# ConvFFN of a two-layer hybrid encoder: 19 of 22 up-projection column pairs by Strassen's seven block products, the down projection as a phase of its own

## The chip, the cores and the metric

The kernel runs on one core of a Trainium2 chip. The metric is the device time of one execution in microseconds, as the median of several runs. Five engines work side by side, each through its own list of instructions in a fixed order: TensorE (PE, with its weight loads shown as PEld), VectorE (DVE), ScalarE (ACT), GpSimd (POOL) and SyncE (SP). Semaphores tie them together. Matmuls write PSUM, which has eight banks of 512 columns of fp32; the other engines read them from there.

## The reference

Two layers run over 1024 prompt tokens and 64 sample tokens (1088 in all), width 1024. Each layer has a mixer (gated linear attention beside differential attention) and a causal ConvFFN. The change is in the second half of each layer:

```python
x = x + rms_norm(mix, ln_mix_post)
h = rms_norm(x, ln_ffn_pre)
up = h @ w_ffn_up                        # 1024 -> 2 x 2816
ext = jnp.concatenate([conv_state.astype(up.dtype), up], axis=1)
c = conv_b
for i in range(CONV_W):                  # 3 taps along the tokens
    c = c + conv_w[i] * ext[:, i:i + T]
g, u = jnp.split(c, 2, axis=-1)
y = jax.nn.gelu(g, approximate=True) * u
x = x + rms_norm(y @ w_ffn_down, ln_ffn_post)   # 2816 -> 1024
```

## The kernel before

Activations are kept feature-major: a tile holds 128 features on the partitions and tokens along the free axis. The residual stream and the sums of the down projection live in `ACC` (8 slices k of 128 features x 1088 tokens). Every product is computed as three passes of rounded fp32 parts: high by high, high by low, low by high. So each operand exists twice: `XH`/`XL` for x, `MH`/`ML` for the gated rows y, `WH`/`WL` for four slots of weights. A raw weight block (512 KB) lands in one of two halves of `RAW`; ACT rounds it into `WH`, DVE subtracts for `WL`.

`fm_block` makes 128 output features for one of three token groups (384, 384, 320 tokens): 8 slices x 3 passes = 24 matmuls into one PSUM bank. The up projection has 22 pairs j of such column blocks, a gate block and a value block (s = 0, 1). In the loop at the end of each layer, up pairs alternate with down products: after every second pair, `dn_mms` multiplies the y of two pairs by their rows of `w_ffn_down` (8 blocks m x 3 groups x 6 matmuls), and `ev_dn` adds the result into `ACC`. The last such product takes pairs 18 to 21 and is followed by the norm that ends the layer.

`ffn_step` evicts one up block and advances the two before it: the block leaves PSUM times `RB` (the inverse root mean square of each token, spread over the partitions), the first tap of the convolution runs on ACT, the other two on DVE, gelu on ACT, the gating on DVE, then y is split into `MH` and `ML`.

`chain(l, g, which, tag)` is the residual and norm work of a token group. With which = 1 it stands between the mixer's output projection and the up projection: `ACC` times `RB` plus residual, then `XH`, `XL` and the squares in `SQ`. x goes into the product without its inverse root mean square; `x_norm` computes that meanwhile (`ssum`: three small matmuls `ONE,SQ`; `rstd`: ACT, then a power on POOL; `bcast`: three small matmuls `IDN,RS`; ACT copies to `RB`), and the first blocks of a group are evicted up to five blocks late (`behind`) so that it is ready.

The order of everything is settled when the program is written out: `defer` evicts a block after the next block's matmuls, `pump` takes steps of waiting generators (`beside`, `soon`) by a modelled clock, `need` and `drain` take as many steps at once as are needed, `want` rounds weights. On the chip each engine runs its list as it stands. The helper lines 103 (matmul), 107 (transpose) and 122 (DVE) stand for nearly all instructions of their engines; in the changed file they are 110, 114 and 129.

## Time and profile before

| what | value |
|---|---|
| median of three runs | 2812.64 us (2810.19 to 2818.26) |
| profiled execution | 2810.27 us, span 2808.5 us |
| PE busy | 2766.1 us, 98% of the span |
| DVE busy | 1690.2 us, 60% |
| ACT busy | 1151.0 us, 41% |
| POOL busy | 234.8 us, 8% |
| DMA | 235.46 MB, mean 84 GB/s |
| granted PE clock, first-layer feed-forward | 1.00 |

Busy time is summed over the engine's instructions; a share is of the span. The profile's page gives these, the chain of work that ended last, and groups of instructions by line, operation and tile. The timeline lists single instructions or runs of equal ones with start, length, engine, line, operation, tiles written and read, and count; in brackets stands the idle time ahead of it and what ended it.

### The profile page before, as it was taken

What the parts mean: (1) busy time and instruction counts of PE and PEld (TensorE: products, weight loads), DVE (VectorE), ACT (ScalarE), POOL (GpSimd) and SP (SyncE); (2) the same over time, 40 slices, a digit from 0 to 9 for tenths busy, and PEclk for the clock granted to TensorE, in tenths of its full rate; (3) what the DMA queues carried; (4) which work ended last, traced back from release to release, by engine and by line L of the source; (5) the groups of instructions that cost most, each with busy time, mean ns of one, the idle gap of its engine ahead of it and who ended that gap; (6) DMA issues with size and microseconds to landing.
All of it is one profiled execution on the core that took longest, in us unless ns stands there. A gap on an engine that the chain in (4) does not pass through costs nothing.

```text
span 2808.5 us, 46577 instructions
## 1 busy us (share of the span) xinstructions
PE 2766.1 (98%) x18407; PEld 2710.2 (96%) x18407; DVE 1690.2 (60%) x4104; ACT 1151.0 (41%) x2432; POOL 234.8 (8%) x387
## 2 busy tenths in 40 slices
PE   8999999999999999999999999999999999999999
PEld 8999988999999999999999999889999999999999
DVE  5443458477566666666772433674766666666665
ACT  5334348555322222222454242684552222222235
POOL 2200024200000000000021001340000000000000
PEclk9999999999999999999999999999999999999999
DMA  7421175341111111111362213734311111111122
GB/s 252 137 70 46 58 195 144 117 135 57 46 46 42 42 45 46 46 46 46 109 199 85 62 39 106 203 93 131 122 56 42 42 45 46 46 46 46 46 91 84
DMA packets 250689, 235.46 MB, mean 84 GB/s; under 512 B 12974, under 2 KB 225416, under 8 KB 250472
## 3 DMA queue, kind: packets, MB, share of 16 engines
q1 hardware_dynamic: 233032, 189.62, 23.6%
q0 software_dynamic: 10656, 39.07, 4.0%
q10 hardware_dynamic: 6784, 3.81, 0.5%
q8 instruction: 145, 2.38, 0.4%
q14 instruction: 72, 0.59, 0.1%
HBM read 174.34 MB, written 58.11 MB: 83 GB/s over the span
## 4 chain that ended last, share of the span: by engine, by line
PE 92%; DMA 2%; DVE 2%; issue 2%; ACT 1%; POOL 0%; SPq 0%; ACTq 0%; DVEq 0%; POOLq 0%
PE PS L103 89%; PE PS L107 3%; DVE SML L122 1%; DMA out_dram<-TMP 1%; DVE ACC L122 1%; DMA WH<-QSd 0%; ACT ACC L1070 0%; DMA WH<-KSd 0%; DMA VSd<-TMP 0%; DMA QSd<-MH 0%; DVE TMP L122 0%; ACT WH L275 0%; DVE ML L122 0%; SPq L992 0%; DMA ACC<-in_x_prompt_dram 0%
## 5 line engine op out<-in xcount | busy, mean ns | idle before, releaser
L103 PE MATMUL PS<-XL,WH 128*128 128x384 f32 (+1 forms) x2976 | 558.6, 326 | 0.0
L103 PEld LDWEIGHTS PS<-XL,WH 128*128 128x128 f32 x2976 | 500.7, 188 | 0.0
L103 PE MATMUL PS<-XH,WH 128*128 128x384 f32 (+1 forms) x2592 | 484.9, 328 | 2.8 <-DVE TMP L122 2.8
L103 PE MATMUL PS<-XH,WL 128*128 128x384 f32 (+1 forms) x2592 | 480.0, 326 | 0.0
L103 PEld LDWEIGHTS PS<-XH,WH 128*128 128x128 f32 x2592 | 434.1, 188 | 4.0 <-DVE TMP L122 3.7
L103 PEld LDWEIGHTS PS<-XH,WL 128*128 128x128 f32 x2592 | 434.6, 188 | 0.2
L103 PE MATMUL PS<-MH,WH 128*128 128x384 f32 (+1 forms) x1248 | 387.3, 329 | 0.0
L103 PE MATMUL PS<-MH,WL 128*128 128x384 f32 (+1 forms) x1248 | 385.1, 327 | 0.0
L103 PE MATMUL PS<-ML,WH 128*128 128x384 f32 (+1 forms) x1248 | 384.3, 327 | 0.0
L122 DVE TENSOR_TENSOR TMP<-PS,RB 128x384 f32<-128x384 f32 (+2 forms) x376 | 159.5, 444 | 343.6 <-PE PS L103 329.4
L275 ACT ACTIVATE WH<-RAW 128x1024 fp32r<-128x1024 f32 (+2 forms) x209 | 216.7, 1048 | 336.4 <-PE PS L103 301.3
L1237 ACT ACTIVATE TMP<-TMP,VC 128x384 f32<-128x384 f32 (+1 forms) x264 | 183.1, 693 | 404.4 <-DVE TMP L122 403.6
L122 DVE TENSOR_TENSOR ACC<-PS,ACC 128x384 f32<-128x384 f32 (+1 forms) x456 | 239.6, 533 | 133.6 <-PE PS L103 132.9
L122 DVE TENSOR_TENSOR WL<-RAW,WH 128x1024 fp32r<-128x1024 f32 (+2 forms) x209 | 253.7, 1215 | 99.2 <-ACT WH L275 99.1
L122 DVE SCALAR_TENSOR_TENSOR TMP<-TMP,VC 128x384 f32<-128x384 f32 (+1 forms) x528 | 311.5, 590 | 0.1
L103 PEld LDWEIGHTS PS<-MH,WL 128*128 128x128 f32 x1248 | 230.9, 188 | 0.0
L103 PEld LDWEIGHTS PS<-ML,WH 128*128 128x128 f32 x1248 | 230.9, 188 | 0.0
L103 PEld LDWEIGHTS PS<-MH,WH 128*128 128x128 f32 x1248 | 230.1, 188 | 0.7 <-issue 0.3
L103 PE MATMUL PS<-WH,XH 128*128 128x256 f32 (+1 forms) x864 | 128.8, 292 | 0.0
L122 DVE TENSOR_REDUCE SML<-PS 128x1 f32<-128x384 f32 (+6 forms) x144 | 104.1, 724 | 40.4 <-PE PS L103 38.8
L103 PE MATMUL PS<-WH,XL 128*128 128x256 f32 (+1 forms) x864 | 122.7, 285 | 0.0
L1258 ACT ACTIVATE MH<-TMP 128x384 fp32r<-128x384 f32 x132 | 67.0, 508 | 135.5 <-DVE TMP L122 135.4
(202 smaller groups left out, 3420.3 us busy)
## 6 DMA issues: line engine op xcount, KB each, us to landing
RAW<-in_w_ffn_up_dram SPq DMA_DIRECT2D x88, 512.0 KB
RAW<-in_w_in_dram SPq DMA_DIRECT2D x48, 512.0 KB
RAW<-in_w_ffn_down_dram SPq DMA_DIRECT2D x44, 512.0 KB
RAW<-in_w_out_dram SPq DMA_DIRECT2D x32, 512.0 KB
XH<-XS SPq DMA_DIRECT2D x8, 1536.0 KB
XS<-ACC POOLq DMA_DIRECT2D x6, 1536.0 KB, 6.8
XH<-KSd SPq DMA_DIRECT2D x32, 256.0 KB
XH<-XS SPq DMA_DIRECT2D x4, 1280.0 KB
```

Of the source, the lines that this page charges most:

```text
L103: nc.tensor.matmul(out, lhsT, rhs, **kw)
L107: nc.tensor.transpose(out, in_, idn)
L122: return op(out, *a, **kw)
L275: act(hi, src, AF.Copy)
L1237: act(c, e[:, 0:w], AF.Identity, bias=cb(l, u), scale=cw(l, 0, u))
L1258: act(MH[:, mid["j"] % 4, mid["t0"]:mid["t0"] + n], y[:, :n], AF.Copy)
```

## The change

Three of 22 pairs (j = 0, 1, 2) keep the plain blocks. For the other 19, the 1024 x 256 weights of a pair (gate and value columns) are taken as a 2 x 2 block matrix (features 0 to 511 and 512 to 1023, gate and value), x as a 2 x 2 block matrix (the same feature halves; tokens 0 to 543 and 544 to 1087), and the product is made from seven block products (Winograd's form of Strassen's scheme) in place of eight. Each product is two halves of 272 tokens x 12 matmuls. The sums of weight blocks (four per pair) are made on DVE (`prep`), the sums of x's blocks once per layer (`fresh`, `late_split`), the sums of products in the evictions (`evict`).

The sums need x with its norm applied, so `chain` with which = 1 now makes two passes: the first for residual and squares, then a wait for `x_norm`, then x times weight and `RB`, rounded by ACT, low part by DVE. The eviction of an up block is a plain copy on ACT. The gated rows go to DRAM (`YD`) from POOL's queue. The down projection follows all up products: five rounds over 4, 4, 4, 3 and 3 pairs (`part_mms`, weights of one m in units of 256 or 192 KB), y read back and split, then the last part over pairs 18 to 21 as before.

```diff
+NC = 3
+HT = T // 2
+Q = HT // 2
+NP = 7 * (NF - NC)
+SKIPS = (0, 1, 2)
+CHUNKS = ((0, 4), (4, 8), (8, 12), (12, 15), (15, 18))
...
+        for j in range(NC):
+            L["up", j] = fm_unit(w_ffn_up[l], j * 128, nxt())
+            fm_unit(w_ffn_up[l], FF + j * 128, nxt())
+        L["prod"] = [nxt() for _ in range(NP)]
+        for c, (ja, jb) in enumerate(CHUNKS):
+            for m in range(8):
+                L["dnc", c, m] = part_unit(w_ffn_down[l], ja, jb, m, nxt())
+            nxt(c in SKIPS)
+        held.update((L["dnc", 0, 0], L["dnc", 0, 1]))
+        for j in range(18, NF):
+            L["dn", j] = down_unit(w_ffn_down[l], j * 128, nxt())
...
+        if which == 1:
+            for k in range(8):
+                V.tensor_tensor(a(k), a(k), rb, ALU.mult)
+                V.scalar_tensor_tensor(a(k), a(k), ln(l, which, k), f(XH[:, k, t0:t0 + n]), ALU.mult, ALU.add)
+                if k > 1:
+                    V.tensor_tensor(sq, sq, sqb[:, (k - 1) % 2, :n], ALU.add)
+                act(sqb[:, k % 2, :n] if k else sq, a(k), AF.Square)
+                if k % 4 == 3:
+                    nc.gpsimd.dma_start(XS[:, k - 3:k + 1, t0:t0 + n], accv[:, k - 3:k + 1, t0:t0 + n])
+                if k == 7:
+                    V.tensor_tensor(sq, sq, sqb[:, 1, :n], ALU.add)
+                    soon(x_norm(), (tag, "rs", g))
+                yield
+            while (tag, "rs", g) not in done:
+                yield tag, "rs", g
+            def low(k):
+                x = XH[:, k, t0:t0 + n]
+                V.tensor_tensor(XL[:, k, t0:t0 + n], a(k), f(x), ALU.subtract)
+            for k in range(8):
+                V.scalar_tensor_tensor(a(k), a(k), ln(nl, nw, k), rb, ALU.mult, ALU.mult)
+                act(XH[:, k, t0:t0 + n], a(k), AF.Copy)
+                if k:
+                    low(k - 1)
+                if k == 7:
+                    low(7)
+                    done.add((tag, "x", g))
+                yield
+            return
...
-                V.tensor_tensor(e[:, 2:2 + n], PS[:, b, :n], RB[:, t0:t0 + n], ALU.mult)
+                act(e[:, 2:2 + n], PS[:, b, :n], AF.Copy)
...
-                act(MH[:, mid["j"] % 4, mid["t0"]:mid["t0"] + n], y[:, :n], AF.Copy)
-                mid["y"] = y
+                nc.gpsimd.dma_start(YD[mid["j"], :, mid["t0"]:mid["t0"] + n], y[:, :n])
...
+    def fresh(l):
+        for k in range(4):
+            b11, b12 = accv[:, k, :HT], accv[:, k, HT:]
+            b21, b22 = accv[:, k + 4, :HT], accv[:, k + 4, HT:]
+            V.tensor_tensor(b11, b12, b11, ALU.subtract)
+            act(MH[:, k, :HT], b11, AF.Copy)
+            yield
+            V.tensor_tensor(b12, b22, b12, ALU.subtract)
+            V.tensor_tensor(b22, b22, b11, ALU.subtract)
+            act(MH[:, k, HT:], b22, AF.Copy)
+            yield
+            V.tensor_tensor(ML[:, k, :HT], b11, f(MH[:, k, :HT]), ALU.subtract)
+            V.tensor_tensor(b21, b21, b22, ALU.subtract)
+            yield
+            V.tensor_tensor(ML[:, k, HT:], b22, f(MH[:, k, HT:]), ALU.subtract)
+            yield
+        done.add(("fresh", l))
...
+    def late_split(i):
+        k = i % 4
+        if i < 4:
+            src, hi, lo = accv[:, k, HT:], T3[:, 0, k], T3[:, 1, k]
+        else:
+            src, hi, lo = accv[:, k + 4, :HT], XH[:, k, HT:], XL[:, k, HT:]
+        act(hi, src, AF.Copy)
+        return lambda: V.tensor_tensor(lo, src, f(hi), ALU.subtract)
...
+        def prep(self, p):
+            n, i = divmod(p, 7)
+            if n >= self.n:
+                return
+            a, b = [r.rearrange("p (k c) -> p k c", k=8) for r in self.raw(n)]
+            a11, a12, a21, a22 = a[:, :4], a[:, 4:], b[:, :4], b[:, 4:]
+            s1, s2, s4, s3 = SG
+            src = (a11, s2, s1, s4, s3, a12, a22)[i]
+            if i == 1:
+                V.tensor_tensor(s1, a21, a22, ALU.add)
+                V.tensor_tensor(s2, s1, a11, ALU.subtract)
+            if i == 3:
+                V.tensor_tensor(s4, a12, s2, ALU.subtract)
+            if i == 4:
+                V.tensor_tensor(s3, a11, a21, ALU.subtract)
+            hi, lo = [x.rearrange("p (k c) -> p k c", k=4) for x in self.part(p)]
+            act(hi, src, AF.Copy)
+            self.lows[p] = (lo, src, f(hi))
+        def low(self, p):
+            if p in self.lows:
+                V.tensor_tensor(*self.lows.pop(p), ALU.subtract)
+        def rhs(self, i, k, hl, s):
+            X, M = (XH, XL)[hl], (MH, ML)[hl]
+            c = slice(s * Q, s * Q + Q)
+            d = slice(HT + s * Q, HT + s * Q + Q)
+            return (X[:, k, c], M[:, k, d], M[:, k, c], X[:, k + 4, d], T3[:, hl, k, c], X[:, k + 4, c], X[:, k, d])[i]
+        def mms(self, p):
+            n, i = divmod(p, 7)
+            w = self.part(p)
+            for s in range(2):
+                b = self.bank(p) + s
+                j = 0
+                for wl, hl in PASSES:
+                    for k in range(4):
+                        mm(PS[:, b, :Q], w[wl][:, k * 128:(k + 1) * 128], self.rhs(i, k, hl, s),
+                           start=j == 0, stop=j == 11)
...
+        def evict(self, p):
+            if p < 0:
+                return
+            n, i = divmod(p, 7)
+            b = self.bank(p)
+            out = PS[:, b:b + 2, :Q]
+            if i == 0:
+                act(two(P1S), out, AF.Copy)
+            elif i == 1:
+                V.tensor_tensor(two(U2S), out, two(P1S), ALU.add)
+            elif i == 2:
+                V.tensor_tensor(two(U4S), out, two(U2S), ALU.add)
+            elif i == 3:
+                self.second(0, b, U4S)
+            elif i == 4:
+                self.second(1, b, U4S)
+                V.tensor_tensor(two(U2S), out, two(U2S), ALU.add)
+            else:
+                s = i - 5
+                V.tensor_tensor(two(EB[s][:, 2:2 + HT]), out, two((P1S, U2S)[s]), ALU.add)
+                self.ends(s, n)
...
+        def conv(self, p):
+            n, i = divmod(p, 7)
+            if i == 6 and n < self.n:
+                self.tap(0, 0, n)
+            n -= 1
+            if n < 0 or i > 4:
+                return
+            if i == 0:
+                self.tap(1, 0, n)
+                self.tap(0, 1, n)
+            elif i == 1:
+                self.tap(0, 2, n)
+            elif i == 2:
+                act(CB[0], CB[0], AF.Gelu_apprx_tanh)
+                self.tap(1, 1, n)
+            elif i == 3:
+                self.tap(1, 2, n)
+            else:
+                y, c = CB
+                V.tensor_tensor(y[:, :SEQ], y[:, :SEQ], c[:, :SEQ], ALU.mult)
+                V.tensor_tensor(y[:, SEQ:T], y[:, SEQ + 2:T + 2], c[:, SEQ + 2:T + 2], ALU.mult)
+                nc.gpsimd.dma_start(YD[NC + n], y[:, :T])
...
+        blk = Blocks(l)
+        for j in range(2, NC):
+            for g in range(3):
+                for s in range(2):
+                    up_block(j, s, g)
+                    if j + 1 < NC:
+                        if g == 0:
+                            want(L["up", j] + 2 + s)
+                    elif (g, s) == (0, 0):
+                        blk.load(0)
+                    elif (g, s) == (1, 1):
+                        blk.prep(0)
+                    elif (g, s) == (2, 0):
+                        need(("fresh", l))
+                        drain()
+                        blk.low(0)
+                        blk.prep(1)
+                    pump(2)
+        blk.low(1)
+        blk.start()
+        for p in range(NP):
+            n, i = divmod(p, 7)
+            blk.mms(p)
+            if p == 0:
+                flush()
+                blk.load(1)
+                blk.prep(2)
+                blk.low(2)
+            elif p < 3:
+                ffn_step(l, None)
+            if p == 4:
+                for e in EB:
+                    V.memset(e[:, 0:2], 0.0)
+            blk.evict(p - 1)
+            blk.prep(p + 3)
+            blk.conv(p)
+            if p < 4:
+                lows2 = [late_split(2 * p), late_split(2 * p + 1)]
+                for x in lows2:
+                    x()
+            blk.low(p + 3)
+            if i == 4:
+                blk.load(n + 2)
+            if n == blk.n - 1:
+                d0 = L["dnc", 0, 0]
+                ys = TMP[:, 544:544 + T]
+                if i == 0:
+                    y_load(0, ys)
+                elif i == 3:
+                    y_high(0, ys)
+                    y_low(0, ys)
+                    y_load(3, ys)
+                elif i == 4:
+                    y_load(1, RB)
+                    y_load(2, SQ)
+                    held.difference_update((d0, d0 + 1))
+                    fetch(d0 + 1)
+                elif i == 5:
+                    want(d0)
...
+        left = [lambda: (blk.evict(NP - 1), blk.conv(NP))]
+        left += [lambda p=p: blk.conv(p) for p in range(NP + 1, NP + 5)]
+        for c, (ja, jb) in enumerate(CHUNKS):
+            nx = range(*CHUNKS[c + 1]) if c + 1 < len(CHUNKS) else range(18, NF)
+            for m in range(8):
                 for g in range(3):
-                    for s in range(2):
-                        up_block(j, s, g)
-                        if g == 0:
-                            want(n + 2 + s)
-            elif j < 18:
-                for m in range(8):
-                    for g in range(3):
-                        b = bank()
-                        dn_mms(b, j, (j, j + 1), m, g, True, True)
-                        defer(lambda m=m, g=g, b=b, j=j: ev_dn(j == 0, False, m, g)(b))
-                    if m in (1, 4):
-                        want(n + 2 + (m > 1))
+                    b = bank()
+                    part_mms(b, c, m, g)
+                    if left:
+                        left.pop(0)()
+                    defer(lambda m=m, g=g, b=b, c=c: ev_dn(c == 0, False, m, g)(b))
+                    if g == 0:
+                        want(L["dnc", c, m] + 2)
```

Three places in the order of instructions show what moved. The first is PE at the start of the up projection of token group 1, in layer 0. Names: `XH,WH` and the like are the passes of up blocks, `ONE,SQ` and `IDN,RS` the small products of `x_norm`. Before, from the third block of group 0:

```order
L103 MATMUL PS<-XH,WH 128x384 x8
L103 MATMUL PS<-XL,WH 128x384 x8
L103 MATMUL PS<-XH,WL 128x384 x8
L103 MATMUL PS<-ONE,SQ 128x1 x3
L103 MATMUL PS<-XH,WH 128x384 x8
L103 MATMUL PS<-XL,WH 128x384 x8
L103 MATMUL PS<-XH,WL 128x384 x8
L103 MATMUL PS<-IDN,RS 128x128 x3
L103 MATMUL PS<-XH,WH 128x384 x8
L103 MATMUL PS<-XL,WH 128x384 x8
L103 MATMUL PS<-XH,WL 128x384 x8
```

and now:

```order
L110 MATMUL PS<-XH,WH 128x384 x8
L110 MATMUL PS<-XL,WH 128x384 x8
L110 MATMUL PS<-XH,WL 128x384 x8
L110 MATMUL PS<-XH,WH 128x384 x8
L110 MATMUL PS<-XL,WH 128x384 x8
L110 MATMUL PS<-XH,WL 128x384 x8
L110 MATMUL PS<-ONE,SQ 128x1 x3
L110 MATMUL PS<-IDN,RS 128x128 x3
L110 MATMUL PS<-XH,WH 128x384 x8
L110 MATMUL PS<-XL,WH 128x384 x8
L110 MATMUL PS<-XH,WL 128x384 x8
```

The block that stood between the two small products of `x_norm` stands ahead of both, and the blocks behind them read `XH` and `XL` of the same group.

The second is DVE in the chain of token group 2. `ACC<-ACC,RB` and `ACC<-ACC,VC,XH` are the residual, `XL` the low part of x, `SQ` the squares, `TMP` the convolution's steps. Before, the chain stood among the evictions of group 0's blocks:

```order
L122 TENSOR_TENSOR ACC<-ACC,RB 128x320
L122 SCALAR_TENSOR_TENSOR ACC<-ACC,VC,XH 128x320
L122 SCALAR_TENSOR_TENSOR XL<-ACC,VC,XH 128x320
L122 TENSOR_TENSOR SQ<-SQ,TMP 128x320
L122 MEMSET TMP 128x2
L122 TENSOR_TENSOR TMP<-PS,RB 128x384
L122 SCALAR_TENSOR_TENSOR TMP<-TMP,VC 128x384
L122 COPY HALO<-TMP 128x2
L122 SCALAR_TENSOR_TENSOR TMP<-TMP,VC 128x384
L122 TENSOR_TENSOR ACC<-ACC,RB 128x320
L122 SCALAR_TENSOR_TENSOR ACC<-ACC,VC,XH 128x320
L122 SCALAR_TENSOR_TENSOR XL<-ACC,VC,XH 128x320
```

and now it begins behind the step for the third block of group 1 (the first three rows), in one piece of 36 rows of which these are the first:

```order
L129 COPY HALO<-TMP 128x2
L129 SCALAR_TENSOR_TENSOR TMP<-TMP,VC 128x384
L129 TENSOR_TENSOR TMP<-TMP 128x384
L129 TENSOR_TENSOR ACC<-ACC,RB 128x320
L129 SCALAR_TENSOR_TENSOR ACC<-ACC,VC,XH 128x320
L129 TENSOR_TENSOR ACC<-ACC,RB 128x320
L129 SCALAR_TENSOR_TENSOR ACC<-ACC,VC,XH 128x320
L129 TENSOR_TENSOR ACC<-ACC,RB 128x320
L129 SCALAR_TENSOR_TENSOR ACC<-ACC,VC,XH 128x320
L129 TENSOR_TENSOR SQ<-SQ,TMP 128x320
```

and these are where the second pass begins, behind the last squares:

```order
L129 SCALAR_TENSOR_TENSOR ACC<-ACC,VC,XH 128x320
L129 TENSOR_TENSOR SQ<-SQ,TMP 128x320 x2
L129 SCALAR_TENSOR_TENSOR ACC<-ACC,VC,RB 128x320 x2
L129 TENSOR_TENSOR XL<-ACC,XH 128x320
L129 SCALAR_TENSOR_TENSOR ACC<-ACC,VC,RB 128x320
L129 TENSOR_TENSOR XL<-ACC,XH 128x320
```

Each slice is handled in two passes, and no eviction stands between their rows.

The third is DVE ahead of the first block product; `ACC<-ACC 128x544` and `ML<-ACC,MH` are `fresh`, `WL<-RB,WL` is the low part of the first product's weights. Before, evictions of the up blocks of pair 2 stood here alone (`TMP<-PS,RB`), for example:

```order
L122 COPY TMP<-HALO 128x2
L122 TENSOR_TENSOR TMP<-PS,RB 128x384
L122 SCALAR_TENSOR_TENSOR TMP<-TMP,VC 128x384
L122 COPY HALO<-TMP 128x2
L122 TENSOR_TENSOR ML<-TMP,MH 128x384
L122 SCALAR_TENSOR_TENSOR TMP<-TMP,VC 128x384
```

and now, behind the step for the second block of group 1 of pair 2 (the first two rows), the end of `fresh` follows in one piece:

```order
L129 COPY HALO<-TMP 128x2
L129 SCALAR_TENSOR_TENSOR TMP<-TMP,VC 128x384
L129 TENSOR_TENSOR ACC<-ACC 128x544 x2
L129 TENSOR_TENSOR ML<-ACC,MH 128x544
L129 TENSOR_TENSOR ACC<-ACC 128x544
L129 TENSOR_TENSOR ML<-ACC,MH 128x544
```

and, after more of the same, up to the weights:

```order
L129 TENSOR_TENSOR ACC<-ACC 128x544 x3
L129 TENSOR_TENSOR ML<-ACC,MH 128x544
L129 TENSOR_TENSOR ACC<-ACC 128x544
L129 TENSOR_TENSOR ML<-ACC,MH 128x544
L129 TENSOR_TENSOR WL<-RB,WL 128x512
L129 TENSOR_TENSOR ACC<-SQ 128x4x128
L129 TENSOR_TENSOR ACC<-ACC,RB 128x4x128
L129 COPY TMP<-HALO 128x2
```

The weights' low part and the first weight sums (`128x4x128`) stand behind all of `fresh`.

215 lines of the change are left out of this document (143 added, 72 removed).

## The prediction

> **What bounds the kernel now.** I read the page's busy shares first, then the chain that ended last, then the stretch of one feed-forward part.
>
> ```profile
> PE 2766.1 (98%) x18407; PEld 2710.2 (96%) x18407; DVE 1690.2 (60%) x4104; ACT 1151.0 (41%) x2432; POOL 234.8 (8%) x387
> 527.56 834.85 PE PS L103 x5088
> 1910.04 834.92 PE PS L103 x5088
> core 0: us, PE busy (x) PEld busy (x) DVE busy (x) ACT busy (x) POOL busy (x), PEclk, DMA share, GB/s
> 613.76:1395.00 781.24, 780.80 (x4747) 780.34 (x4745) 515.75 (x1297) 257.96 (x412) 5.63 (x6) 1.00 0.18 53
> ```
>
> TensorE (PE) is busy 98% of the span. The two rows of the chain (start, length) are the output projection and feed-forward of each layer: 835 us with nothing on the chain but matmuls. In the window, the feed-forward of layer 0, PE stands still for 0.4 of 781 us, VectorE (DVE) works 66% of it and ScalarE (ACT) 33%. So a matmul saved there is time saved, and a PE that waits there is time lost. This execution took 2810.27 us (span 2808.5); the median of the three runs is 2812.64, 2.4 more.
>
> **What the products save.** The pitch of PE's instructions is read from the starts of the weight loads in the timeline (start, length, count at the end): first 384-column matmuls, then 320, and then the only stage with 272, the first value projection.
>
> ```profile
> 1003.25 1.40 PEld L103 LDWEIGHTS PS<-XL,WH 128*128 128x128 f32 x8
> 1004.63 1.40 PEld L103 LDWEIGHTS PS<-XH,WL 128*128 128x128 f32 x8
> ...
> 1016.70 1.22 PEld L103 LDWEIGHTS PS<-XH,WL 128*128 128x128 f32 x8
> 1017.88 1.21 PEld L103 LDWEIGHTS PS<-XH,WH 128*128 128x128 f32 x8
> ...
> 102.75 1.06 PEld L103 LDWEIGHTS PS<-WH,XL 128*128 128x128 f32 x8
> 103.75 1.06 PEld L103 LDWEIGHTS PS<-WL,XH 128*128 128x128 f32 x8
> ```
>
> Eight take 1.387 us over a longer run of such rows (1.38 here), 1.174 (1.18) and 1.00: 173.4, 146.7 and 125.1 ns each. A plain pair is 48 matmuls in each of three groups: 48 x (2 x 0.1734 + 0.1467) = 23.69 us. A Strassen pair is 7 products x 2 halves x 12 = 168 of 272 columns: 168 x 0.1251 = 21.02 us. That is 2.67 us a pair, and for 19 pairs in 2 layers **-101.5 us**. The down projection keeps all its matmuls and widths (1584 a layer), so on PE its part saves nothing; its accumulation into ACC falls from ten rounds to six, on a DVE that hid it.
>
> **Is a Strassen pair still bound by PE?** DVE's pitch from a dense stretch of starts:
>
> ```profile
> 611.04 0.55 DVE L122 TENSOR_TENSOR ACC<-ACC,RB 128x384 f32<-128x384 f32 x1
> 611.51 0.61 DVE L122 SCALAR_TENSOR_TENSOR ACC<-ACC,VC,XH 128x384 f32<-128x384 f32 x1
> 612.04 0.60 DVE L122 SCALAR_TENSOR_TENSOR XL<-ACC,VC,XH 128x384 fp32r<-128x384 f32 x1
> 612.57 0.55 DVE L122 TENSOR_TENSOR SQ<-SQ,TMP 128x384 f32<-128x384 f32 x1
> 613.04 1.21 DVE L122 TENSOR_TENSOR WL<-RAW,WH 128x1024 fp32r<-128x1024 f32 x1
> 613.32 0.75 PE L103 MATMUL PS<-XL,WL 128*128 128x320 f32 x4
> 613.90 1.58 PE L103 MATMUL PS<-XH,WH 128*128 128x384 f32 x8
> 614.17 0.48 DVE L122 TENSOR_TENSOR SQ<-SQ,TMP 128x320 f32<-128x320 f32 x1
> ```
>
> A two-input operation starts the next one 0.47 us later at 384 elements and 1.13 (613.04 to 614.17) at 1024, so 1.03 ns an element: 0.60 at 512, 0.635 at 544, 0.40 at 320. The scalar form is 0.53 at 384, 1.26 at 1090. Per pair DVE has 4 weight sums and 7 low parts (11 x 0.60), 5 whole evictions (3.2), 2 in three pieces (1.6), 4 taps (5.0), the gating (1.3) and 6 two-column copies (0.6): 18.3 us of PE's 21.0. ACT has less than half of that: seven 512-copies, two first taps, gelu and one eviction. Products take PSUM banks in four double sets, so DVE may fall two products behind. I cost this at nothing; the bounds are 0, and about 1 us a pair if each of the 34 operations costs its full length (0.08 more than its pitch, 21.0 in all) and waits come on top.
>
> **What the new order of the normalisation costs.** T0 is 613.90, the first up-projection matmul; PE had no gap there. Before, the up-projection read unnormalised x (rstd came in at the eviction), so a block needed one pass over the residual; group 1's pass ran beside the output projection. Now a block needs two passes with the squared norm between, and group 1's first pass stands behind T0 (the order of DVE in the change section). What lies between the last square and a usable RB:
>
> ```profile
> 627.78 0.72 PE L103 MATMUL PS<-ONE,SQ 128*128 128x1 f32 x6
> 628.54 0.26 ACT L423 ACTIVATE RS<-PS,EPC 128x3 f32<-128x3 f32 x1 [3.34 <-PE PS L103]
> 628.90 1.02 POOL L424 TENSOR_TENSOR RS<-RS,NEGH 128x3 f32<-128x3 f32 x1 [7.98 <-ACT RS L423]
> 632.62 0.83 PE L103 MATMUL PS<-IDN,RS 128*128 128x128 f32 x6
> 633.49 0.49 ACT L433 ACTIVATE RB<-PS 128x384 f32<-128x384 f32 x1 [4.68 <-PE PS L103]
> 633.87 0.55 ACT L485 ACTIVATE XH<-ACC,VC 128x320 fp32r<-128x320 f32 x1
> ```
>
> 0.76 + 0.36 + 1.02 + 0.87 + 0.49, then one scalar operation (0.53) and one copy to XH (0.62 at 384): 4.7, with handovers 5 us. In before a whole block of matmuls stood between the two small products (628.5 to 632.6 is that block); in the changed order of PE they stand next to each other, with nothing to cover these 5 us.
> Group 0: its second pass ends 2.4 us after T0 (five DVE operations after the last output eviction), so PE waits 2.4; four blocks of 24 x 0.1734 = 4.16 and the small products end at T0 + 20.2.
> Group 1: first pass 8 x (0.47 + 0.53 + 0.47) = 11.8 us on DVE, mixed with the taps of blocks that have to end first (the last such step at about 17, six and a half us of the pass after it): done at about T0 + 25, normalised at 30. The second pass gives PE one slice k per 1.0 us (0.53 + 0.47), so the first block ends at 30 + 8.7 + 1.5 = 40.3 and not at 22.0: 18 us lost so far.
> Group 2: its two passes stand in one piece behind the step that evicts group 1's third block, which is done at about 50. 8 x (0.40 + 0.47 + 0.40) = 10.2, the norm 5, 8 x (0.47 + 0.40) = 7.0: its first block ends at about T0 + 74, against 39 without waits. **+35 us a layer** in all. Ends: 20, if a third of DVE's work finds room earlier than I place it; 45, if every operation takes its length and not its pitch.
>
> **What the entry to Strassen costs.** Of the 24 operations of 544 elements that build x's block sums, one stands earlier and 23 in one piece behind the step for the last block of group 1 of pair 2, ahead of the low part of the first product's weights: 23 x 0.635 + 0.6 = 15.2 us, of which PE's last two blocks (7.0, less 1.2 for the eviction) cover 5.8 and the first eight matmuls of the product 1.0. **+8.5**; ends 4 and 12. Behind it the next low part waits too, 3.3 us of DVE against 3.0 of PE: nothing.
>
> **What the entry to the down phase costs.** Rows 1 to 3 of y come back from DRAM and are split (a 1024-element hi takes ACT 1049 ns, a low part DVE 1218, in the groups below), and the first two weight units with them, in the last three products, behind evictions and a first tap.
>
> ```profile
> L122 DVE TENSOR_TENSOR WL<-RAW,WH 128x1024 fp32r<-128x1024 f32 x64 | 77.9, 1218 | 14.6 <-ACT WH L275 14.6
> L275 ACT ACTIVATE WH<-RAW 128x1024 fp32r<-128x1024 f32 x63 | 65.3, 1049 | 150.1 <-PE PS L103 150.1
> ```
>
> Three splits on one engine behind the other, a tap and two weight halves are 6 to 7 us more than the last product's 3.0 covers; less if the loads are early. I take **+6.5**, ends 2 and 10. Inside the phase each weight unit has 12 x 0.493 = 5.9 us of PE (9 to 12 matmuls in each of three groups) for 0.6 + 1.9 us of DVE and as much ACT: no wait. The way through DRAM is 24.5 MB a layer, some 33 GB/s beside the 53 of the window row: hidden. XS now leaves in two transfers a group and each y in one, on POOL's queue, whose power operation (L424) would wait for an issue of some 0.9 us; the first is issued four slices ahead, the second together with the last squares, behind PE's 0.76 and ACT's 0.36. The loads of raw weights stay on SP, with as many bytes as before.
>
> **The clock.** An idle PE comes back slowly here. The rows are windows of PE and the weight loads after the stop at 376 to 380.
>
> ```profile
> 378.00:380.00 2.00, 0.00 (x0) 0.74 0.35 98
> 380.00:382.00 2.00, 1.86 (x7) 0.50 0.02 4
> 382.00:384.00 2.00, 2.00 (x10) 0.50 0.55 196
> ...
> 381.37 2.10 PEld L103 LDWEIGHTS PS<-XH,WL 128*128 128x128 f32 x8
> 383.41 2.20 PEld L103 LDWEIGHTS PS<-XL,WH 128*128 128x128 f32 x8
> ```
>
> The granted clock is 0.50, and 16 matmuls of 320 columns take 4.17 us in place of 2.35: 1.8 lost for one stop. Four stops a layer (groups 1 and 2, Strassen, down) are new. In the first two PE is paced by DVE anyway while the clock is low (three matmuls at half clock, 1.04 us, for a slice of 1.0), so I count 0.5 there and 2 at the others: **+10** for both layers; ends 0 and 16.
>
> [...]
>
> **Sum.** 2810.3 - 101.5 + 2 x (35 + 8.5 + 6.5) + 10 = 2818.8; with the runs' median above this execution, 2820. The change saves matmuls and gives the time back as waits at four places.
>
> **Rivals.**
> A gain: the waits are half of what I count, because the dependences let the passes run closer than I place them by hand (for it: DVE is idle a third of this stretch, and I price first blocks slice by slice; against it: DVE executes in the written order, and the two passes are 19 and 17 us of it). With 25 to 30 a layer: 2810 - 101.5 + 55 + 5 = 2770.
> Strassen is bound by DVE (for it: 18.3 of 21.0 with every wait for PE or ACT excluded; against it: two products of slack). It decides from 2.7 us a pair more than I count; each us beyond is 38 in all: at 1 us, 2858, slower.
> The clock: half speed also holds through the paced blocks and they no longer keep up, 4 us more for each of four such blocks and 2 more at each other stop: 2820 + 24 = 2844, slower (for it: the row of 2.20 us; against: 1.04 fits 1.0).
> The change does nothing: no saving on PE, if 272 columns cost more where x is the moving operand and every weight load is new. The value stage has the same widths and fresh loads, 1.00 for 8; I give this no share of its own.
>
> **How the numbers follow.** Forecast (waits as summed, 2798 to 2842) 0.46; gain 0.29; DVE 0.14; clock 0.11. About 0.3% is what a measurement here tells from no change: 2804 to 2821. From the forecast 0.08 lies below that, 0.14 in it and 0.24 above; the gain puts 0.27 below and 0.02 in it; the others lie above. Faster 0.35, same 0.16, slower 0.49. The range reaches from the gain's 2762 to DVE's 2862; the forecast's own is 2798 to 2842.
>
> **What would show it.** In the profile after: a pair's products at 1.00 us for eight matmuls and 21.0 us a pair with PE idle under 1%; between the output projection and the first product about 50 us of PE idle or slow time a layer, with DVE (ACC, XL) and ACT (XH, RB) as releasers and two stops of about 10 us; a stop of about 8 before the first product with DVE ML or WL as releaser; one of some 6 at the first down block; PEclk 0.5 behind them. I am wrong if the stops of groups 1 and 2 are below 20 us together, or if PE waits within the pairs.

## The result: 1.5% slower, and the profile after

The changed kernel takes 2856.81 us (median of 4 runs, 2852.97 to 2860.20), the kernel before 2812.31 beside it: ratio 1.0154, 95% interval 1.0134 to 1.0174. The profiled execution has a span of 2855.1 us. The forecast was 2820 with a range of 2762 to 2862.

The first lines are from the page of after: the busy times. Then one window each, of before and of after: the first layer from its first up-projection matmul (T0) to the first squared norm at its end (busy time of PE, PEld, DVE, ACT and POOL with counts, granted clock, DMA share, GB/s).

```profile
PE 2717.5 (95%) x19319; PEld 2641.3 (93%) x19319; DVE 1798.5 (63%) x3632; ACT 1205.4 (42%) x2468; POOL 268.4 (9%) x449
```

```profile
613.90:1373.10 759.20, 759.20 (x4614) 759.01 (x4613) 497.58 (x1260) 247.01 (x390) 4.78 (x5) 1.00 0.18 55
```

```profile
614.50:1388.50 774.00, 730.74 (x5070) 720.55 (x5069) 559.86 (x1042) 280.79 (x422) 20.80 (x35) 0.96 0.27 86
```

PE's busy time fell by 48.6 us and the span grew by 46.6. In the window PE was never idle before; now it stands still for 43.3 of 774.0 us. Its busy time there fell by 28.5 us and not by the 50.7 that the matmuls save: the other 22 I put down to matmuls that come one by one (in the rows below such a one of 384 columns is 0.44 us long at a clock of 1.00 and 0.69 at 0.50, where eight in a row take 1.38 at 1.00, from 658.90 to 660.28) or run at a lower clock (0.96 in the mean of this window, 1.00 before). Its waits in that window, by what ended them (total us, times, longest):

```profile
PE PS L110 <- DVE SQ L129: 15.1, 2, 8.7
PE PS L110 <- DVE WL L129: 12.7, 3, 9.3
PE PS L110 <- ACT XH L513: 9.0, 16, 1.8
PE PS L110 <- POOL RS L436: 2.6, 2, 1.3
PE PS L110 <- ACT WH L290: 2.1, 1, 2.1
```

`SQ`, `RS` and `XH` are the new normalisation (27 us), `WL` is the low part of weights ahead of the first product (9.35) and of the first down block (3.15). The timeline of PE shows group 1 and then group 2 of that normalisation (start, length, idle time ahead and what ended it):

```profile
641.57 1.44 PE L110 MATMUL PS<-ONE,SQ 128*128 128x1 f32 x6 [6.34 <-DVE SQ L129]
644.32 1.65 PE L110 MATMUL PS<-IDN,RS 128*128 128x128 f32 x6 [1.31 <-POOL RS L436]
647.76 1.22 PE L110 MATMUL PS<-XH,WH 128*128 128x384 f32 x2 [1.79 <-ACT XH L513]
649.44 0.69 PE L110 MATMUL PS<-XH,WH 128*128 128x384 f32 x1 [0.46 <-ACT XH L513]
...
654.91 2.75 PE L110 MATMUL PS<-XL,WH 128*128 128x384 f32 x8
657.47 1.59 PE L110 MATMUL PS<-XH,WL 128*128 128x384 f32 x8
658.90 1.55 PE L110 MATMUL PS<-XH,WH 128*128 128x384 f32 x8
...
680.28 1.44 PE L110 MATMUL PS<-ONE,SQ 128*128 128x1 f32 x6 [8.74 <-DVE SQ L129]
683.04 1.65 PE L110 MATMUL PS<-IDN,RS 128*128 128x128 f32 x6 [1.31 <-POOL RS L436]
686.36 1.10 PE L110 MATMUL PS<-XH,WH 128*128 128x320 f32 x2 [1.67 <-ACT XH L513]
...
696.06 1.19 PE L110 MATMUL PS<-XH,WH 128*128 128x320 f32 x7
```

Each stop is followed by matmuls that come one by one, one for each slice k that has been rounded. The granted clock is 0.50 there, from 640.5 to 657.5 and from about 674.6 to 695. The row that starts at 658.90 is group 1's second block, so its first ended at T0 + 44.4; group 2's ended at 696.06, T0 + 81.6. The forecast had T0 + 40.3 and T0 + 74. Then the first product, still PE's timeline, and one window of 20 us in the middle of the products:

```profile
730.82 0.66 PE L110 MATMUL PS<-XL,WL 128*128 128x272 f32 x4
740.83 2.18 PE L110 MATMUL PS<-XH,WL 128*128 128x272 f32 x8 [9.35 <-DVE WL L129]
742.81 1.11 PE L110 MATMUL PS<-XL,WL 128*128 128x272 f32 x4
```

```profile
1000.00:1020.00 20.00, 20.00 (x162) 20.00 (x161) 17.62 (x34) 7.28 (x11) 0.53 (x1) 1.00 0.25 82
```

Inside the pairs PE is busy 20.00 of 20 us, at full clock, beside a DVE of 88%. A pair takes 21.0 us. The rows at the entry to the down phase, first PE, then DVE's split of row 0 of y, SyncE's queue (SP) and ACT's first split of weights:

```profile
1146.56 0.44 PE L110 MATMUL PS<-MH,WH 128*128 128x384 f32 x1 [2.08 <-ACT WH L290]
1150.33 0.69 PE L110 MATMUL PS<-MH,WL 128*128 128x384 f32 x1 [3.15 <-DVE WL L129]
```

```profile
1135.02 1.29 DVE L129 TENSOR_TENSOR ML<-TMP,MH 128x1088 fp32r<-128x1088 f32 x1
1136.33 0.34 SPq L1488 DMA_DIRECT2D TMP<-YD  x1
1136.84 0.32 SPq L1488 DMA_DIRECT2D RB<-YD  x1
1137.25 0.38 SPq L1488 DMA_DIRECT2D SQ<-YD  x1
1137.68 1.04 SPq L251 DMA_DIRECT2D RAW<-in_w_ffn_down_dram  x2
1145.88 0.63 ACT L290 ACTIVATE WH<-RAW 128x512 fp32r<-128x512 f32 x1 [12.19 <-DMA RAW<-in_w_ffn_down_dram]
```

The load of row 3 of y (into `TMP`) waits until row 0 has been split there (1136.31); rows 1 and 2 and the weights stand behind it in SP's queue, and all four leave within 1.4 us of one another. ACT begins on the first weights 8.2 us after their issue and has stood idle for 12.19 us until then.

By stages, from the starts of such rows, in us (the two layers agree within 0.5):

| stage | before | after | without the waits | forecast loss | loss |
|---|---|---|---|---|---|
| up projection to the first product, one layer | | 116.3 | 71.1 (3 x 23.69) | 35 | 45, or 42.5 |
| products | | 413.5 | 399.4 (19 x 21.02) | 8.5 | 14 |
| down phase to the first `ONE,SQ` | | 244.2 | 235.2 (with another entry, measured below) | 6.5 | 9 |
| feed-forward, whole | 759.2 | 774.0 | | | |
| mixer of layer 1 (from there to the next T0) | 623.3 | 638.9 | | 0 | 15.6 |

The 71.1 leave out the small products of the norm, which the forecast's times hold; counted as the forecast counts, by the end of group 2's first block, the first loss is 42.5. The 235.2 still hold two waits of 1.3 us together.

The last row was not in the sum at all. All of its 15.6 us lie ahead of the first squared norm beside the output projection (`ONE,SQ`, at 1935.13 before and 1966.11 after: 562.0 and 577.6 us into the mixer), and in that part no instruction of PE, DVE or ACT changed its place in its engine's order. The last 61.3 us up to T0, in which DVE already has the new passes, take the same in both.

### The profile page after: what moved, and what is told of

It reads as the page before. It is cut to its first block, busy times and chain, and to the rows that moved or that the text cites. A ratio compares the mean times of both kernels' runs of the same rounds, so it can differ in the third digit from the quotient of the medians.

```text
span 2855.1 us, 48522 instructions
## 1 busy us (share of the span) xinstructions
PE 2717.5 (95%) x19319; PEld 2641.3 (93%) x19319; DVE 1798.5 (63%) x3632; ACT 1205.4 (42%) x2468; POOL 268.4 (9%) x449
## 5 line engine op out<-in xcount | busy, mean ns | idle before, releaser
L110 PE MATMUL PS<-XH,WL 128*128 128x272 f32 (+2 forms) x3728 | 688.6, 304 | 18.7 <-DVE WL L129 18.7
L110 PE MATMUL PS<-MH,WL 128*128 128x272 f32 (+2 forms) x1936 | 399.7, 305 | 6.3 <-DVE WL L129 6.3
L110 PEld LDWEIGHTS PS<-XL,WH 128*128 128x128 f32 x1680 | 301.3, 193 | 0.0
L110 PEld LDWEIGHTS PS<-XH,WH 128*128 128x128 f32 x1296 | 232.1, 192 | 36.6 <-ACT XH L513 30.1
L129 DVE TENSOR_TENSOR WL<-RAW,WH 128x1024 fp32r<-128x1024 f32 (+3 forms) x177 | 167.8, 949 | 130.8 <-ACT WH L290 130.8
L110 PE MATMUL PS<-XL,WL 128*128 128x272 f32 (+2 forms) x1408 | 242.0, 294 | 0.0
L110 PE MATMUL PS<-MH,WH 128*128 128x384 f32 (+1 forms) x720 | 218.3, 335 | 9.4 <-ACT WH L290 4.5
L110 PE MATMUL PS<-ML,WH 128*128 128x384 f32 (+1 forms) x720 | 215.5, 332 | 1.3 <-DVE ML L129 1.3
L129 DVE SCALAR_TENSOR_TENSOR ACC<-ACC,VC 128x1090 f32<-128x1090 f32 x152 | 204.5, 1346 | 0.1
L110 PEld LDWEIGHTS PS<-XL,WL 128*128 128x128 f32 x1408 | 204.6, 189 | 0.0
```

Of the source, the lines that this page charges most:

```text
L110: nc.tensor.matmul(out, lhsT, rhs, **kw)
L129: return op(out, *a, **kw)
```

## The experiments

My theory after the two traces: the products save what was worked out, and the time is lost at four places that are each a matter of order and not of work: the normalisation of groups 1 and 2, DVE's block sums ahead of the first product, SP's queue at the down entry, and other PSUM banks in layer 1's mixer. The rivals stand with each run. Ratios are to the kernel before, measured beside each run, with 95% intervals.

**One product pair instead of 19.** Is the saving on PE real?

```diff
-NC = 3
+NC = 21
-SKIPS = (0, 1, 2)
+SKIPS = (0,)
```

> 21 plain pairs and one by block products: the new chain, the rows through DRAM and the down phase stay, nearly all of the saving in matmuls is given up, and the block sums have 18 pairs to be taken beside. Theory (a pair by products saves PE 2.67 us and is bound by PE): against the run with five plain pairs (2823.9), 16 pairs x 2 layers x 2.67 = 85 us more, about 2909; the up part without products then takes as long as before plus the stops of groups 1 and 2. Rival (products lose part of it to DVE): 50 us more or less, about 2870.

In this kernel row 0 of y is loaded into `TMP` while, by the written order, the last plain pair's convolution still works there, so that pair's values are not the program's; no work is left out.

2918.3 us, 1.0377 [1.0364, 1.0391]. The rival falls. Up projection and products together take 563.6 us in a layer, against 521.0 with five plain pairs (below): 42.6 us for 16 pairs, 2.66 each. The whole is 94 us longer than with five plain pairs and not 85, mostly since the down phase has become 4.7 us longer in each layer, with its entry behind a single product pair.

**The normalisation's latency.** x isn't normalised afresh: `x_norm` and the wait for it are left out and the second pass multiplies by what `RB` holds.

```diff
-                    soon(x_norm(), (tag, "rs", g))
+                    done.add((tag, "rs", g))
...
-            while (tag, "rs", g) not in done:
-                yield tag, "rs", g
```

> The second norm of x is left out: x_norm with its small products, its ACT and POOL step and the wait for it are gone; the second pass multiplies by what still stands in RB. All DVE passes stay. Theory (the stops of groups 1 and 2 are DVE work plus a bare norm of 5 to 6 us each that nothing covers): 2 x 5.5 us a layer and some half-clock time go, 22 to 30 us in all, about 2830. Rival 1 (DVE's two passes alone set these stops, the norm lies beside other DVE work): less than 8 us. Rival 2 (the wait for the norm is the whole stop): 70 us or more.

2831.67 us, 1.0067 [1.0055, 1.0079], 25 us less than the changed kernel and inside the 22 to 30 expected. By the profiles the feed-forward is 9 and 10 us shorter in the two layers; the rest lies outside it and isn't shown to come from this edit. So the squared norm and its way through PE, ACT and POOL is a fifth of the 45 us. In its waits of one layer `SQ` and `RS` are gone and `XH` has taken their place, 21.9 us for 26.7 of the three:

```profile
PE PS L110 <- ACT XH L511: 21.9, 15, 9.7
```

DVE's two passes are the larger part and hold PE up with or without the norm.

**The second pass later.** The blocks of pairs 0 and 1 read unnormalised x, as in the kernel before, and are multiplied by `RB` at eviction; normalising follows a group's blocks, ahead of pair 2. (With three plain pairs the first raw weights land in `RB` before groups 1 and 2 are scaled, so their scale is another here.)

```diff
-        if which == 1:
...  (both passes at once, removed)
+    def renorm(l, g, tag):
...  (the second pass alone)
-            need((tag, "x", g))
+            need((tag, "x" if j < 2 else "xn", g))
...
+            beside(renorm(l, g, tag))
...
+        beside(fresh(l))
```

> The second pass of the norm is moved. The chain is one pass again, as before: pairs 0 and 1 read unnormalised x and get the inverse root mean square at the eviction (up to five blocks late); a group's x is scaled in ACC and rounded anew for XH and XL only behind that group's blocks of pairs 0 and 1, ahead of pair 2, and the block sums follow. DVE's work is the same but for 12 evictions that it does in place of ACT. Theory (groups 1 and 2 stop for two passes and a bare norm; 42 us a layer): these stops go; DVE has some 20 us more to do than PE up to the first product, which now wait in pieces ahead of pair 2 and of the first product: 20 to 35 us less a layer, about 2800. Rival (DVE's whole work up to the first product sets its start, whatever the order): the first product starts within 8 us of the changed kernel's 116 us after T0, time above 2840.

2816.35 us, 1.0011 [1.0001, 1.0020], against some 2800 expected. The up projection is 20 us a layer shorter, the low end of the theory's 20 to 35, and 25 are left; the rival (8 us at most) falls. The trace has them: PE's waits are now a 4.68 for the first `XH`, the slices one by one behind it, and a longer stop ahead of the first product:

```profile
671.85 0.69 PE L110 MATMUL PS<-XH,WH 128*128 128x384 f32 x1 [4.68 <-ACT XH L523]
...
722.99 2.18 PE L110 MATMUL PS<-XH,WL 128*128 128x272 f32 x8 [11.34 <-DVE WL L129]
```

The pass was moved but stayed one piece, and a piece of DVE work that the next matmul needs stops PE at its new place too.

**Five plain pairs.** Cover for the block sums (`fresh`) ahead of the first product.

```diff
-NC = 3
+NC = 5
-SKIPS = (0, 1, 2)
+SKIPS = (0, 1, 2, 3, 4)
```

> Five plain pairs in place of three, 17 by block products; the block sums of x have two more pairs to be taken beside. Theory (the stop ahead of the first product, 9.4 us and some 4 us of half clock a layer, is the burst of sums): it goes nearly whole, 12 a layer, against 2 x 2.67 us that two more plain pairs cost: 13 us less in all, about 2844. Rival (the modelled clock puts the sums in one piece again, or DVE has no room): the stop stays and the pairs cost 10.7 us, about 2867.

2823.85 us, 1.0046 [1.0034, 1.0058], 33 us less than the changed kernel where 13 were expected. The stop before the first product is gone and the products take 357.3 us, 17 x 21.02, so all 14 us of their entry came from it. 9.2 and 8.0 us a layer remain as gain after two plain pairs more; 13 of the rest are layer 1's mixer (625.8 us), since this edit happens to shift the banks as well.

**The down entry.** The first weights are fetched four products earlier, and row 3 of y is loaded behind rows 1 and 2.

```diff
                     y_load(0, ys)
+                    held.difference_update((d0, d0 + 1))
+                    fetch(d0 + 1)
                 elif i == 3:
                     y_low(0, ys)
-                    y_load(3, ys)
                 elif i == 4:
                     y_load(2, SQ)
-                    held.difference_update((d0, d0 + 1))
-                    fetch(d0 + 1)
+                    y_load(3, ys)
```

> Entry of the down phase: the first two weight units are fetched in the first product of the last pair (before: the fifth), and the load of row 3, which has to wait for the low part of row 0 on the same staging tile, is issued behind the loads of rows 1 and 2 and no longer ahead of them in SP's queue. Theory (the stop of 11 us a layer is loads that stand behind a waiting load in SP's queue): it falls to about 5, 10 to 12 us less in all, about 2846. Rival (rows 1 and 2 can't be loaded before RB and SQ are free, and ACT's and DVE's splits set the end): 0 to 3 us less.

2838.95 us, 1.0090 [1.0077, 1.0103], 18 us less than the changed kernel where 10 to 12 were expected. In the first layer the phase takes 235.2 us for 244.2; of the waits of 2.08 and 3.15 two short ones are left, both for the low part of y:

```profile
1148.01 0.45 PE L110 MATMUL PS<-ML,WH 128*128 128x384 f32 x1 [0.89 <-DVE ML L129]
1149.21 0.45 PE L110 MATMUL PS<-ML,WH 128*128 128x384 f32 x1 [0.40 <-DVE ML L129]
```

In the second layer it takes 237.1 for 244.5, with waits of 0.33, 0.88 and 0.41 us. Another 4 us of the 18 lie in layer 1's mixer (634.6 us for 638.9), which this edit doesn't touch. Which of the two changes of order does more isn't shown, since no run has one of them alone.

**The stops filled.** Matmuls whose result nobody reads fill PE's stops at groups 1 and 2 and in the first product.

```diff
+        def fill(n):
+            for _ in range(n if which == 1 and g else 0):
+                nc.tensor.matmul(PS[:, 5, 128:512], XH[:, 0, 0:128], XH[:, 1, 0:384], start=True, stop=True)
...
+                    if p == 0 and s == 0 and wl:
+                        for _ in range(45):
+                            nc.tensor.matmul(PS[:, 6 if b < 6 else 5, 128:512], ...)
```

> Matmuls on old data into an unused part of a PSUM bank fill most of PE's stops, so that none lasts 3 us: 24 and 40 of 384 columns ahead of the small products of groups 1 and 2, 4 and 6 behind them, 45 in the first product where it waits for the low part of its weights. They fit into the stops (4.2 of 6.3 us, 6.9 of 8.7, 7.8 of 9.4). Theory (after each such stop PE runs at half clock, which costs 2.5 us each in groups 1 and 2 and 2.5 to 4 at the first products): 7 to 9 us a layer less, about 2841. Rival (the half clock lies beside waits for DVE and ACT and costs nothing): no change within 3 us.

2857.07 us, 1.0158 [1.0145, 1.0171]: no change, the rival. From the first product to the down phase it takes 413.5 us in both layers, as in the changed kernel. Windows of 2 us at the end of the stop and behind it, after first, this run second, and then PE's timeline of this run:

```profile
740.00:742.00 2.00, 1.17 (x5) 1.17 (x6) 1.97 (x4) 0.00 (x0) 0.00 (x0) 0.50 0.00 0
742.00:744.00 2.00, 2.00 (x11) 2.00 (x11) 1.66 (x8) 1.71 (x5) 0.00 (x0) 0.50 0.00 0
```

```profile
740.00:742.00 2.00, 1.63 (x13) 1.64 (x14) 1.97 (x6) 0.33 (x1) 0.00 (x0) 1.00 0.00 0
742.00:744.00 2.00, 1.66 (x14) 1.43 (x12) 1.66 (x6) 1.84 (x6) 0.00 (x0) 1.00 0.00 0
```

```profile
740.37 1.27 PE L110 MATMUL PS<-XH,WL 128*128 128x272 f32 x8 [1.53 <-DVE WL L129]
...
744.67 1.27 PE L110 MATMUL PS<-MH,WL 128*128 128x272 f32 x8 [1.01 <-DVE WL L129]
```

The clock is 1.00 in place of 0.50, and PE reaches the next product early and waits there for its weights. What sets the pace behind this stop is DVE, not the clock. At group 1 the clock fell again among the single matmuls behind the filler: they are 0.44 us long at first and 0.69 later, which are the lengths that the changed kernel has at 1.00 (the row at 1146.56) and at 0.50 (at 649.44). Both kinds came 1.00 us apart. What the blocks behind them lose isn't shown: in layer 1 the way to the first product became 4.4 us longer with the filler, 120.8 for 116.4, and its mixer 2.8 shorter, so the equal time of the whole is in part chance. At the down entry it wasn't tried.

**The banks.** `ring["i"]` hands out PSUM banks in turn. At the start of layer 1 it stands at 498 in the kernel before and at 146 in the changed one, which sets it anew behind its products (`ring["i"] = (2, 4, 0, 0)[blk.bank(NP - 1) // 2]`), so blocks of the same order find other banks. Two runs, one for each direction; no instruction is added or moved in either. First the changed kernel with the old count, then the kernel before with the new one:

```diff
+        ring["i"] = 498 if l else ring["i"]
```

> Only the rotation of the PSUM banks is changed: the counter is set at the start of layer 1 to the value that it has in the kernel before. In the changed kernel the first output-projection block of layer 1 that needs fresh weights waits 3.6 us for a DVE operation (XL from PSUM), where the kernel before waits for ACT alone; the theory is that this block lands in a bank that the DVE operation still reads. Theory: the stop goes and with it some half-clock time, 4 to 7 us off 2856.8, about 2851. Rival (layer 1's mixer is later only by the phase of the clock and by DMA): no change beyond 1.5 us.

```diff
+        ring["i"] = 146 if l else ring["i"]
```

> The kernel before with one line added: at the start of layer 1 the counter that hands out PSUM banks is set to 146, where the changed kernel has it, in place of 498. No instruction is added, removed or moved. Theory (the changed kernel's mixer of layer 1 is longer because its blocks find other banks, on which PE then waits for other evictions): layer 1's mixer grows from 623.3 to some 634 to 639 us and the time by 10 to 15, to about 2823. Rival (the longer mixer comes from something that layer 0's products or down phase leave behind, and setting the counter cured it there by chance): within 3 us of before.

The first: 2843.87 us, 1.0111 [1.0098, 1.0124], 13 us less than the changed kernel, about twice what I expected; the mixer takes 628.1 for 638.9. The second: 2819.9 us, 1.0027 [1.0015, 1.0039], 8 us more than the kernel before; its mixer takes 631.2 for 623.3. So the banks cost 8 to 11 us of the mixer's 15.6, and the rival falls, though with less than the 10 to 15 expected. One of the new waits is a block of the output projection; the rows are from PE's timeline of before, of after, and of before with the new count:

```profile
1910.04 0.98 PE L103 MATMUL PS<-MH,WH 128*128 128x384 f32 x4
```

```profile
1939.46 0.97 PE L110 MATMUL PS<-MH,WH 128*128 128x384 f32 x4 [3.61 <-DVE XL L129]
```

```profile
1914.40 1.46 PE L103 MATMUL PS<-MH,WH 128*128 128x384 f32 x4 [3.44 <-DVE XL L122]
```

With the new count PE waits at this block for a piece of DVE's work, and with the old one it has no wait there. The order of the instructions with what each waits for shows this before any run: a wait for DVE stands in this place where the kernel before has one for ACT. Over all profiles here the mixer of layer 1 takes 623.3 to 628.2 us in the six with the count at 498 and 631.3 to 641.6 in the six with 146 (the two runs that change nothing but the number of pairs stand at 144). So the count sets the larger part; what moves the mixer by 5 to 10 us inside each group stays open.

**All four edits together** (the later pass, five plain pairs, the down entry, the old count).

> Four edits together: the second pass behind pairs 0 and 1, five plain pairs, the early fetch and the reordered loads at the entry of the down phase, the bank rotation of before. Theory (the four waits and the bank rotation are what the change lost): of some 68 us a layer of stops 15 to 20 stay, 5.3 are paid for two plain pairs, and the 13 us of the rotation come back: about 2755, below both kernels. Rival (what one stop releases another takes, on a DVE that is the bound up to the first product): about 2800.

2782.2 us, 0.9890 [0.9875, 0.9904]: faster than both kernels, but 27 us above the theory's 2755 and nearer to the rival's 2800. The normalisation ahead of pair 2 still stops PE: 11.3 us of waits for `XH` in one layer, the longest 4.3.

**The second pass in small pieces.** The scaling of `ACC` by `RB` is spread beside pairs 0 to 3, with evictions times `RB` until then; `XH` and `XL` are made group by group behind pair 3's blocks, and `fresh` behind that.

```diff
+    def scale(l, g, tag):
+        t0, n = GROUPS[g]
+        while (tag, "rs", g) not in done:
+            yield tag, "rs", g
+        for k in range(8):
+            V.scalar_tensor_tensor(accv[:, k, t0:t0 + n], accv[:, k, t0:t0 + n], ln(l, 2, k),
+                                   RB[:, t0:t0 + n], ALU.mult, ALU.mult)
+            yield
...
+                        if j == NC - 2 and s:
+                            beside(renorm(l, g, tag))
+                            if g == 2:
+                                beside(fresh(l))
```

> All four edits together, with the normalisation spread out: five plain pairs whose evictions multiply by RB; the scaling of ACC by the inverse root mean square (24 DVE operations) beside plain pairs 0 to 3, its rounding into XH and XL behind the blocks of pair 3, the block sums behind those; the down entry and bank rotation as in the all-together run (2782.2). Theory (what is left of the loss there, about 12 us a group 1 and 2 in each layer, is DVE's scaling and rounding in one burst ahead of a block): those bursts go, 2 x 20, and up to 2 x 10 come back because the block sums now end later, just ahead of the first product: about 2760, between 2745 and 2775. Rival (the stops there are latencies of ACT's rounding and of PE's clock, not of DVE's burst): no more than 8 us better than 2782.

> As the run before it, but with seven plain pairs in place of five (15 by products), so that the block sums have two more pairs of matmuls to lie beside. Two pairs fewer by products cost 2 x 2 x 2.67 = 10.7 us. Theory (the block sums in front of the first product stop PE for some 10 us a layer with five plain pairs, and two more pairs cover them): about 2755, 5 us or more better than with five. Rival (nothing is left to cover there): 10 us slower than with five plain pairs.

With five plain pairs 2754.54 us, 0.9807 [0.9790, 0.9825], inside the 2745 to 2775 expected; with seven 2764.13, 0.9837 [0.9820, 0.9853]. PE has no wait left from T0 to the first product. There both stop, for 11.36 and 11.05 us (the rows of the run with five and of the one with seven): `fresh` is now the last thing, in one piece again.

```profile
749.95 2.18 PE L110 MATMUL PS<-XH,WL 128*128 128x272 f32 x8 [11.36 <-DVE WL L129]
```

```profile
794.65 2.18 PE L110 MATMUL PS<-XH,WL 128*128 128x272 f32 x8 [11.05 <-DVE WL L129]
```

The second run shows my theory of cover wrong in this form. Its expectation's rival has the number (10 us slower), but not the reason: there was something to cover, yet two pairs more don't help when the written order puts the block sums into the last pair however many there are. DVE had room: in the run with seven it was busy 11.8 to 16.2 us in each of the four windows of 20 us ahead of the stop.

**The block sums one pair earlier.** Seven plain pairs; rounding behind pair 4, and up to four steps behind a block in place of two.

```diff
-            need((tag, "x" if j < NC - 1 else "xn", g))
+            need((tag, "x" if j < NC - 2 else "xn", g))
...
-                        if j == NC - 2 and s:
+                        if j == NC - 3 and s:
...
-                    pump(2)
+                    pump(2 if j < NC - 2 else 4)
```

> Seven plain pairs as in the run before, where PE still stopped 11.05 us ahead of the first product, because the block sums stood in one piece behind the rounding in the last plain pair, however many pairs there were. Now the rounding stands one pair earlier (behind the blocks of pair 4), the blocks of pairs 5 and 6 read normalised x, and up to four steps in place of two are taken behind a block of these pairs, so that the block sums are spread over the last pair and a half. Theory (the stop is DVE's order, not its amount of work): the stop of 11 us and about 2 us behind it go in both layers, 2764 - 26 = about 2738, between 2732 and 2748. Rival (DVE has no room for these 15 us there, or another step is last ahead of the product): 2755 to 2765.

2743.67 us, 0.9762 [0.9748, 0.9775], 2.4% faster than the kernel before and 4.0% faster than the changed one: the theory. The run has both changes of the order, so how much each of them does isn't shown. Windows ahead of and over the first product, with one piece first and spread second, show the same DVE work at another place:

```profile
760.00:780.00 20.00, 20.00 (x122) 20.00 (x121) 15.79 (x42) 13.44 (x30) 1.08 (x2) 1.00 0.44 124
780.00:800.00 20.00, 8.95 (x52) 8.73 (x51) 19.43 (x38) 7.38 (x14) 0.54 (x1) 0.66 0.02 7
```

```profile
760.00:780.00 20.00, 20.00 (x122) 20.00 (x121) 18.07 (x42) 10.35 (x18) 1.08 (x2) 1.00 0.08 28
780.00:800.00 20.00, 18.03 (x124) 16.32 (x123) 16.00 (x36) 10.74 (x23) 1.08 (x2) 0.98 0.05 19
```

PE loses 2 us in these 20 in place of 11. The products take 320.8 and 319.3 us for 331.0; 315.3 would be 15 x 21.02.

## Why the prediction was right and where it was not

The mechanism was the one forecast: PE gets its matmuls back and returns the time as waits at the places named. The number was 38 us too low, 2818.8 for an execution that took 2856.8. That is above the forecast's own 2798 to 2842; the time lies in the range only because that reaches up to the rival with DVE as the bound, whose mechanism the traces exclude. Being inside is luck. The signs named for the mechanism came: no wait of PE within the pairs, a stop of 9.35 (about 8 was named) ahead of the first product, a clock of 0.50 behind the stops (to 657.5, 695, 746 and 1159 at groups 1 and 2, the first product and the down entry), and waits of 11.5 and 13.3 us in groups 1 and 2 with the short ones between the slices, above the 20 together that were the least; only the releasers there were partly others (`SQ` and `RS` beside `XH`). The 38 us are these.

- **What the products save: right.** 21.0 us a pair as computed, -101.5, and the run with one product pair bears the gain out.
- **Strassen bound by PE: right.** 20.00 of 20 us busy; the priced DVE share, 18.3 of 21.0 or 87%, was 88%. The rival that had DVE as the bound is excluded.
- **The normalisation: mis-sized, 42.5 for 35 a layer.** Group 1's first block ended at T0 + 44.4 for 40.3, group 2's at T0 + 81.6 for 74. Three steps fell short. Group 1's squares were ready at T0 + 27.1 (the row at 641.57) for 25. The way from there to the first matmul on new x took 6.2 and 6.1 us (641.57 to 647.76, 680.28 to 686.36) for 5. And a block ended 11.1 and 9.7 us behind that for 10.3 and about 9: its eight `XL,WH` matmuls, 2.56 us for 1.39, ran at a clock of 0.50 with nothing to wait for. Group 2 inherits all that group 1 is late. The end of 45 was near.
- **Entry to Strassen: mis-sized, 14 for 8.5**, above the end of 12. The sum ended with the first product's weights ("the next low part waits too ...: nothing"). It left out that DVE also carries the last up blocks' steps and eight more 544-element splits (`late_split`) in the first products; DVE is busy 3.6 of the 4 us around the end of the stop (1.97 and 1.66), and with the stop filled the second product waits 1.01 for its weights and the products take no less.
- **Down entry: mis-sized, 9 for 6.5.** I counted splits and not SP's queue, where a load that waits for its buffer held the rows and weights behind it; ACT stood idle for 12.19 us ahead of the first weights. The run with the other entry takes 9.0 and 7.3 us less in the two layers.
- **The clock: +10 was too much.** It does fall to 0.50 as forecast, at the first product from 736 to 746, behind 4.5 us without a matmul. But the price of 2 us at the first product was 0: half speed lay beside DVE's work, and the products take 413.5 us with the clock kept at 1.00 too. The 2 us at the down entry are neither confirmed nor excluded. At groups 1 and 2 it is about 1 us each (eight `XL,WH` matmuls in 2.56 us for 1.39 and in 2.14 for 1.17), inside the 42.5. The rival of 2844 falls: the single matmuls at half clock kept their pitch, 0.69 us of 1.00.
- **Missing: the mixer of layer 1, +15.6.** I compared orders of instructions only in the feed-forward and without what they wait for. The changed kernel sets the bank counter anew in layer 0 and leaves it elsewhere; that is 8 to 11 of the 15.6, and the rest stays open.

Worked through: the three waits are 7.5 + 5.5 + 2.5 = 15.5 a layer above the forecast, with whatever the clock cost in them, so its 5 a layer go: 10.5. Twice that is 21, with the mixer 36.6, and 2818.8 + 36.6 = 2855.4, within 1.4 us of the execution. The terms are measured in this execution, so this shows that they are complete and no more.

## What to carry to other kernels

Work moved off the bound engine is only worth what the order around it lets through: here 51 us a layer were saved on PE and some 66 lost around it, and with 15 pairs by products and the new DVE work cut into pieces and written beside matmuls the kernel became 2.4% faster than before. When a change adds DVE work that a later matmul needs, price it as one piece at the place where the order puts it, and look for room a stage earlier; more matmuls ahead of it are worth nothing while the written order keeps the piece last, as the first run with seven plain pairs shows. And compare, in stages that the change does not touch, what each instruction waits for: a round-robin of buffers that starts elsewhere is a change too.

## What was unexpected

- A bank counter that starts at another value, with the same instructions in the same order, made the kernel before 8 us slower (1.0027) and the changed one 13 us faster.
- Half clock (0.50) behind the stop at the first product was free: with the clock at 1.00 there the products took the same 413.5 us.
- A load that waited for its buffer at the head of SP's queue, with the late weights behind it, cost 9 us a layer; two edits of issue order, no byte less, took back 9.0 us in one layer and 7.3 in the other.
